# Eighty stores of an RWKV-7 layer, issued by ScalarE's queue instead of SP's

## The chip, the cores and the metric

The kernel runs on one core of one Trainium2 chip. The metric is the device time of one execution in microseconds (us); a kernel's time is the median of several executions. TensorE multiplies matrices, VectorE and ScalarE do elementwise work, GpSimd does elementwise work and some DMAs, SyncE (SP) issues most DMAs. SP and ScalarE each have a DMA queue of their own.

## What is computed

A trunk of two layers for 512 positions with a width of 2048, in float32. Layer 0 is a hybrid attention; the change lies in layer 1, an RWKV-7 time mixing. Cut to what matters:

```python
def rwkv7_mixer(h, mu, w_r, w_k, w_v, w_z, w_o, w0, w1, w2, a0, a1, a2, k_k, k_a, ...):
    xx = shifted(h) - h
    xr, xw, xk, xv, xa, xz = [h + xx * mu[i] for i in range(6)]
    r, k, v, z = xr @ w_r, xk @ w_k, xv @ w_v, xz @ w_z
    w = -softplus(-(w0 + tanh(xw @ w1) @ w2)) - 0.5
    decay = exp(-exp(w))
    a = sigmoid(a0 + (xa @ a1) @ a2)
    kk = normalised per head of (k * k_k)
    k = k * (1 + (a - 1) * k_a)
    # per position: state = state * decay + (state @ -kk) (kk * a)^T + v k^T;  y = state @ r
    ...
    return (norm(y) + bonus) * silu(z) @ w_o
```

## The kernel before

Everything is kept with the 2048 features on partitions, as 16 blocks of 128 ("pairs" of two heads of 64), and the 512 positions along the free dimension. A float32 product is made of three matmuls, `mm3` (L116 to L118): each operand is split into a high and a low half. For a weight tile of 128 x 1024, `wload` (L103) issues its load on SP's queue into a `raw` buffer (two of them), ScalarE makes the high half `wh` (L85) and VectorE the low half `wl` (L86), into three buffers each. Weight tiles are numbered through the program; `wh556` is the high half of tile 556.

The stage around the change is the dense part of layer 1, in the trace from 1203 to 1640 us. The generator `dense()` runs the projections with keys (`rwk`), values (`rwv`), receptances (`rwr`) and gates (`rwz`), one block of 128 outputs after another, each of two weight tiles. After each block a function takes the result from PSUM: `stash` for a key block (L915 copies it to `vf`, L916 stores it to `kpd` in HBM), `values` for a value block (L1014 and L1015, to `vfd`). Between these matmuls run the pieces of `pair(p)`, which is the elementwise work of one block of heads. It loads the keys back (L931), squares and normalises them, and computes decays and rates in one long run of ScalarE operations, from `th` (L950) over `ep` (L957) and `em` (L959) to `km` (L967) and `sq`; a text below calls that run the burst of a pair. L960 stores the decays `ep` to `epd`. VectorE forms the products `bk` and `kk` (L977 to L982), stored by SP at L980 and L983. `values` also orders, six ticks later, a `turn()`: TensorE transposes the value block (L1020), ScalarE copies it to `vt` (L1022, a single buffer), and two DMAs store it to `vtd` (L1025). `rates` (L1032) and GpSimd's later stages read `epd`, `vfd` and `vtd` back. `ahead(k)` prepares inputs of the gates (`hin`, `mx`, `xz`, stored at L1010 to `xzd`), and a triangular inverse per four pairs copies its results `pu` to `u4` (L906).

What runs when on TensorE is written by hand: `fill` advances one tick at a time, a tick runs what is due (`at(n, f)`) and then one `mm3` of the dense stream.

```python
tc.manual_schedule(engines={mybir.EngineType.PE})
def fill(n):
    for _ in range(n):
        for f in due.pop(now[0], ()):
            f()
        next(stream, None)
        now[0] += 1
```

The order of the other engines, SP's and ScalarE's queues included, is found by the framework's scheduler. DMAs of SP and ScalarE report their landing to one of eight counters, which the two queues share.

Of the kernel before, what the change touches and what calls it, by code (L numbers as in the profile page):

```python
# [18 lines left out]
P = 128  # L19
# [29 lines left out]
def _trunk(ctx, tc, d, out):  # L49
    nc = tc.nc  # L50
# [26 lines left out]
    def v_(name, i=0, n=1):  # L77
        o = VEC[name] + i
        return vec[:, o:o + n]
# [4 lines left out]
    def split(hi, lo, src):  # L84
        nc.scalar.activation(hi, src, AF.Copy)  # L85
        nc.vector.tensor_tensor(lo, src, f32(hi), op=ALU.subtract)  # L86
# [23 lines left out]
    def bdmm(ps, mat, hi, lo):  # L110

        nc.tensor.matmul(ps, mat, hi, start=True, stop=False)
        nc.tensor.matmul(ps, mat, lo, start=False, stop=True)

    def mm3(ps, ah, al, bh, bl, start, stop_):
        nc.tensor.matmul(ps, ah, bh, start=start, stop=False)  # L116
        nc.tensor.matmul(ps, al, bh, start=False, stop=False)  # L117
        nc.tensor.matmul(ps, ah, bl, start=False, stop=stop_)  # L118
# [115 lines left out]
    with ExitStack() as st0:  # L234
# [14 lines left out]
        for k in range(KT):  # L249
            ada.scale_shift(0, k)  # L250
            t = tp.tile([P, S], F32, tag="t", name=f"t{k}")
# [10 lines left out]
        for j in range(8):  # L262
            t = tp.tile([P, S], F32, tag="t", name=f"lt{j}")
# [12 lines left out]
    with ExitStack() as L0:  # L276
# [285 lines left out]
        with ExitStack() as ml:  # L562
# [68 lines left out]
            def attend(head, vh, vl, qrh, qrl, qk, sz):  # L631
# [31 lines left out]
                nc.sync.dma_start(yd[8 + head], y)  # L663

            nxt = pair(0), [proj(0)]
            for hp in range(4):
                pv_, qk = nxt
# [9 lines left out]
    with ExitStack() as so:  # L677
# [6 lines left out]
        for k in range(KT):  # L684
            t = y2.tile([P, S], F32, tag="yl_", name=f"yld{k}")
            nc.sync.dma_start(t, yd[k])
            a = yp.tile([P, S], R32, name=f"yh{k}")
            b = yp.tile([P, S], R32, name=f"yl{k}")
# [21 lines left out]
    NP, NC_, C = KT, 8, 64  # L710
# [3 lines left out]
    epd, vfd, y2d, z2d = (scr(n, NP, P, S) for n in ("epd", "vfd", "y2d", "z2d"))  # L714
    vtd = scr("vtd", NP, C, NC_, P)
    kpd = scr("kpd", NP, P, S)
# [30 lines left out]
    def sigmoid(t):  # L747

        nc.scalar.activation(t, t, AF.Ln, bias=1.0)
        nc.scalar.activation(t, t, AF.Exp, scale=-1.0)  # L750
# [39 lines left out]
    with ExitStack() as kp:  # L790
# [14 lines left out]
        with pool(name="sp", bufs=2) as sp:  # L805
# [3 lines left out]
            for k in range(KT):  # L809
                h = sp.tile([P, S + 1], F32, tag="h", name=f"hn{k}", bufs=3)  # L810
                nc.gpsimd.memset(h[:, 0:1], 0.0)
                t = sp.tile([P, S], F32, tag="t", bufs=4, name=f"t1_{k}")
# [22 lines left out]
        for i in range(2):  # L835
            t = lp.tile([96, S], F32, tag="lt", name=f"lt{i}")
# [33 lines left out]
        def store(g, U):  # L870
            T = kw.tile([64, 32, 32], F32, tag="t11", name=f"T{g}", bufs=1)
            nc.gpsimd.tensor_copy(T, U[:64].rearrange("p s t -> p t s"))
            nc.gpsimd.dma_start(unu[g], U.rearrange("p s t -> p (s t)"))
            nc.gpsimd.dma_start(unt[g], T.rearrange("p s t -> p (s t)"))
# [38 lines left out]
        def stash(p, ps):  # L913
            t = T_("vf", p)
            nc.scalar.activation(t, ps, AF.Copy)  # L915
            nc.sync.dma_start(kpd[p], t)  # L916

        def pair(p):

            vp = lambda n: v_(n, p)  # L920
            if p % 2 == 0:
                l2[p // 2] = []
                for n_ in ("rw2", "ra2"):
                    raw = lp.tile([96, 256], F32, tag="l2raw", name=f"l2raw{n_}{p}")
                    nc.sync.dma_start(raw, d[n_][:, p * P:(p + 2) * P])
                    hi = lp.tile([96, 256], R32, tag=f"l2h{n_}", name=f"l2h{n_}{p}")
                    lo = lp.tile([96, 256], R32, tag=f"l2l{n_}", name=f"l2l{n_}{p}")
                    split(hi, lo, raw)
                    l2[p // 2].append((hi, lo))
            ps = T_("kp", p)  # L930
            nc.sync.dma_start(ps, kpd[p])  # L931
            yield

            kk = T_("kk", p, bufs=3)
            nc.scalar.activation(kk, ps, AF.Identity, scale=vp("k_k"))
            sq = T_("sq", p)
            nc.scalar.activation(sq, kk, AF.Square)
            sqh, sql = (kw.tile([P, S], R32, tag=f"sq{i}", name=f"sq{i}_{p}", bufs=1) for i in range(2))
            split(sqh, sql, sq)
            yield  # L940
            cs = slice((p % 2) * P, (p % 2 + 1) * P)
            pu_ = []
            for i in range(2):
                u = pl.tile([P, S], F32, tag="pl", name=f"pl{p}{i}")
                mm3(u, *(w[:, cs] for w in l2[p // 2][i]), *lora[i], True, True)
                pu_.append(u)
            pn = pa.tile([P, S], F32, tag="pa", name=f"pn{p}")
            bdmm(pn, bdr, sqh, sql)
            th = T_("th", p, bufs=1)
            nc.scalar.activation(th, pu_[0], AF.Exp, bias=nw0[:, p:p + 1], scale=-1.0)  # L950
            sigmoid(th)
            L = th
            nc.vector.tensor_tensor_scan(L, smask, th, 0.0, op0=ALU.mult, op1=ALU.add)
            ep = T_("ep", p, (P, NC_, C + 1))
            nc.vector.memset(ep[:, :, 0:1], 1.0)
            L3 = L.rearrange("p (c t) -> p c t", t=C)
            nc.scalar.activation(ep[:, :, 1:], L3, AF.Exp, scale=-CE)  # L957
            em = T_("em", p)
            nc.scalar.activation(em, L, AF.Exp, scale=CE)  # L959
            nc.sync.dma_start(epd[p].rearrange("p (c t) -> p c t", t=C), ep[:, :, 1:])  # L960
            nc.vector.tensor_copy(dmp(p), ep[:, :, C])
            ta = T_("ta", p)
            nc.scalar.activation(ta, pu_[1], AF.Exp, bias=nw0[:, 16 + p:17 + p], scale=-1.0)
            sigmoid(ta)

            km = T_("km", p, bufs=1)
            nc.scalar.activation(km, ta, AF.Identity, bias=oka[:, p:p + 1], scale=vp("k_a"))  # L967
            nc.vector.tensor_tensor(km, ps, km, op=ALU.mult)

            nc.vector.tensor_scalar(sq, pn, 1e-24, None, op0=ALU.max)  # L970
            nc.scalar.activation(sq, sq, AF.Ln)
            nc.scalar.activation(sq, sq, AF.Exp, scale=-0.5)
            yield
            nc.vector.tensor_tensor(kk, kk, sq, op=ALU.mult)
            bk = T_("bk", p, (P, NC_, 2, C), bufs=1)
            bh = bk[:, :, 0]
            nc.vector.tensor_tensor(bk[:, :, 1], c3(km), c3(em), op=ALU.mult)  # L977
            nc.vector.tensor_tensor(bh, c3(ta), c3(kk), op=ALU.mult)
            nc.vector.tensor_tensor(bh, bh, c3(em), op=ALU.mult)
            nc.sync.dma_start(bkd[p], bk)  # L980
            kt_ = kk
            nc.vector.tensor_tensor(c3(kt_), c3(kk), ep[:, :, :C], op=ALU.mult)  # L982
            nc.sync.dma_start(krd[p, :, :, 0], c3(kt_))  # L983
            yield

            pn = pa.tile([P, S], F32, tag="pa", name=f"pat{p}")
            for c in range(NC_):
                cc = slice(c * C, c * C + C)
                for u in range(2):
                    r_ = slice(64 * u, 64 * u + 64)  # L990
                    nc.tensor.matmul(pn[r_, cc], bh[r_, c], kt_[r_, cc], start=True, stop=True)
            at_ = T_("at", p, (P, NC_, C), bufs=1)
            nc.vector.tensor_tensor(at_, pn.rearrange("p (c t) -> p c t", t=C), am[:, None, :].to_broadcast([P, NC_, C]), op=ALU.mult)
            nc.sync.dma_start(atd[p // 4, :, p % 4], at_)

            if p % 4 == 3:
                U = inverse(p // 4)
                store(p // 4, U)
                inv = inverse2(p // 4)
                for n in (70, 104, 112):  # L1000
                    at(n, lambda: next(inv, None))
# [10 lines left out]
        def values(p, ps):  # L1012
            vf = kw.tile([P, S], F32, tag="vf", name=f"vf{p}")
            nc.scalar.activation(vf, ps, AF.Copy)  # L1014
            nc.sync.dma_start(vfd[p], vf)  # L1015

            def turn():
                pt = pl.tile([P, S], F32, tag="pl", name=f"pvt{p}")
                for b in range(4):
                    nc.tensor.transpose(pt[:, b * P:(b + 1) * P], vf[:, b * P:(b + 1) * P], ident)  # L1020
                vt = kw.tile([P, S], F32, tag="vt", name=f"vt{p}", bufs=1)
                nc.scalar.activation(vt, pt, AF.Copy)  # L1022
                vv = vtd[p].rearrange("t (b a) f -> a t b f", a=2)
                for a in range(2):
                    nc.sync.dma_start(vv[a], vt[64 * a:64 * a + 64].rearrange("p (b f) -> p b f", f=P))  # L1025

            at(6, turn)

# [50 lines left out]
        def at(n, f):  # L1079
            due.setdefault(now[0] + n, []).append(f)  # L1080
# [8 lines left out]
        for j in range(NK0):  # L1089
            stash(j, acck[j])  # L1090
# [369 lines left out]
```

## Time and profile before

| | |
|---|---|
| median of three runs | 2446.71 us (2438.78 to 2450.34) |
| the profiled execution | 2447.56 us, span 2445.8 us, mean granted TensorE clock 0.966 |
| TensorE busy in the span | 2258.9 us (92%) |
| VectorE, ScalarE, GpSimd busy | 1609.8, 1021.0, 628.4 us |
| the stage with the change, 1203 to 1640 us | 437 us |

The profile is one execution on the chip. Its page lists busy times, the costliest groups of instructions and the DMA issues; the trace behind it answers more closely: the busy time of engines in a stretch, what an engine waited for, and the instructions in order of time. In a row of the timeline, the first number is the start (us from the span's start), the second the duration, and brackets give the idle time before it and what ended that. PE is TensorE, DVE VectorE, ACT ScalarE, POOL GpSimd; SPq is SP's DMA queue.

### The profile page before, as it was taken

Reading aid. Unit: us, or ns where it says so; the run is one execution under the profiler, and the core shown is the slowest. Engines: PE = TensorE matmul, PEld = TensorE weight load, DVE = VectorE, ACT = ScalarE, POOL = GpSimd, SP = SyncE. Lnnn points to the kernel's source line nnn. Section 1 sums busy time; section 2 is a strip of 40 time slices with the busy share of each in tenths; the row PEclk is TensorE's granted clock in tenths of the full one; section 3 lists DMA queues with packets and bytes.
Section 4 is the critical chain, followed back from the end, with each engine's and each line's share of the span. In section 5 each row is a group of like instructions: output and inputs, shape, how many; then the busy total and the mean of one; then the engine's idle time right before and its main releaser. Section 6 shows DMA issues by size and latency. Waiting matters only on the chain. (4 is left out here: it accounts for less than half of the span.)

```text
span 2445.8 us, 38074 instructions
## 1 busy us (share of the span) xinstructions
PE 2258.9 (92%) x14148; PEld 1755.3 (72%) x14148; DVE 1609.8 (66%) x2983; ACT 1021.0 (42%) x1809; POOL 628.4 (26%) x855
## 2 busy tenths in 40 slices
PE   6779999999998989998999889999999999997997
PEld 3567877777776877885688667777667777775786
DVE  6974577777767546727667766853566766675755
ACT  4233344444454443223476667642233444444222
POOL 1110022222231110110005455864323333310111
PEclk9999999999988999999999999999999999998998
DMA  8973554444313238835476789877558654445864
GB/s 317 326 247 117 167 165 155 162 154 158 117 47 114 64 105 301 293 126 188 157 219 207 217 264 279 268 203 205 129 143 243 176 142 130 129 133 184 297 203 138
DMA packets 224380, 452.03 MB, mean 185 GB/s; under 512 B 71489, under 2 KB 85953, under 8 KB 222913
## 3 DMA queue, kind: packets, MB, share of 16 engines
q1 hardware_dynamic: 206146, 400.30, 51.0%
q0 software_dynamic: 15744, 47.20, 7.6%
q8 instruction: 111, 1.82, 0.3%
q10 hardware_dynamic: 2304, 2.10, 0.3%
q14 instruction: 75, 0.61, 0.1%
HBM read 365.88 MB, written 83.63 MB: 184 GB/s over the span
## 5 line engine op out<-in xcount | busy, mean ns | idle before, releaser
L85 ACT ACTIVATE wh<-raw 128x1024 fp32r<-128x1024 f32 (+3 forms) x314 | 313.4, 1000 | 460.5 <-PE ps_r L118 85.6
L86 DVE TENSOR_TENSOR wl<-raw,wh 128x1024 fp32r<-128x1024 f32 (+3 forms) x314 | 372.8, 1189 | 198.1 <-ACT wh L85 192.9
L199 DVE CUSTOM_DVE_ANT_0 adaw<-adaw,sc,mod 128x512 f32<-128x512 f32 (+1 forms) x160 | 161.0, 1009 | 51.6 <-DMA adaw<-in_ada 49.0
L199 DVE CUSTOM_DVE_ANT_0 adaw<-adaw,sc,vec 128x1024 f32<-128x1024 f32 (+1 forms) x96 | 119.3, 1242 | 54.5 <-DMA adaw<-in_ada 54.4
L470 POOL TENSOR_TENSOR pcmn<-csn,cmn 128x128 f32<-128x128 f32 x48 | 25.6, 560 | 394.6 <-ACT pn L291 207.3
L116 PE MATMUL pwo<-xho,wh 128*128 128x512 f32 (+1 forms) x288 | 111.2, 386 | 10.7 <-ACT xho L85 7.7
L116 PE MATMUL ps_v<-xh,wh 128*128 128x512 f32 x256 | 106.3, 415 | 8.7 <-ACT wh L85 6.2
L116 PE MATMUL ps_r<-xh,wh 128*128 128x512 f32 x256 | 110.9, 433 | 0.9 <-ACT vf L1014 0.9
L117 PE MATMUL pwo<-xho,wl 128*128 128x512 f32 (+1 forms) x288 | 107.9, 375 | 4.2 <-DVE wl L86 4.2
L116 PE MATMUL ps_z<-xh,wh 128*128 128x512 f32 x256 | 111.4, 435 | 0.0
L117 PE MATMUL ps_v<-xh,wl 128*128 128x512 f32 x256 | 104.0, 406 | 5.2 <-DVE wl L86 5.2
L118 PE MATMUL pwo<-xlo,wh 128*128 128x512 f32 (+1 forms) x288 | 108.4, 377 | 0.0
L118 PE MATMUL ps_v<-xl,wh 128*128 128x512 f32 x256 | 103.9, 406 | 0.3 <-DVE xl L745 0.3
L116 PE MATMUL pw<-yh,wh 128*128 128x512 f32 x256 | 102.0, 399 | 1.9 <-ACT yh L85 1.7
L118 PE MATMUL ps_r<-xl,wh 128*128 128x512 f32 x256 | 103.8, 405 | 0.0
L117 PE MATMUL ps_r<-xh,wl 128*128 128x512 f32 x256 | 103.3, 404 | 0.0
L117 PE MATMUL pw<-yh,wl 128*128 128x512 f32 x256 | 102.5, 401 | 0.3 <-DVE wl L86 0.3
L118 PE MATMUL pw<-yl,wh 128*128 128x512 f32 x256 | 100.5, 396 | 2.0 <-DVE yl L86 2.0
L118 PE MATMUL ps_z<-xl,wh 128*128 128x512 f32 x256 | 101.4, 396 | 0.0
L117 PE MATMUL ps_z<-xh,wl 128*128 128x512 f32 x256 | 101.2, 396 | 0.0
L867 POOL TENSOR_TENSOR U<-U,Ut 128x30 f32<-128x30 f32 (+14 forms) x120 | 96.1, 801 | 9.1
L865 POOL TENSOR_TENSOR Ut<-U 128x30 f32<-128x30 f32 (+14 forms) x120 | 91.2, 760 | 9.1
(466 smaller groups left out, 6217.8 us busy)
## 6 DMA issues: line engine op xcount, KB each, us to landing
adaw<-in_ada SPq DMA_DIRECT2D x128, 512.0 KB, 6.9
adaw<-in_ada SPq DMA_DIRECT2D x128, 256.0 KB, 3.1
raw<-in_win_b SPq DMA_DIRECT2D x58, 512.0 KB, 3.6
raw<-in_rwo SPq DMA_DIRECT2D x36, 512.0 KB, 4.5
raw<-in_wout SPq DMA_DIRECT2D x32, 512.0 KB, 4.8
raw<-in_rwv SPq DMA_DIRECT2D x32, 512.0 KB, 5.0
raw<-in_rwr SPq DMA_DIRECT2D x32, 512.0 KB, 5.0
raw<-in_rwz SPq DMA_DIRECT2D x32, 512.0 KB, 4.0
```

Of the source, the lines that this page charges most:

```text
L85: nc.scalar.activation(hi, src, AF.Copy)
L86: nc.vector.tensor_tensor(lo, src, f32(hi), op=ALU.subtract)
L116: nc.tensor.matmul(ps, ah, bh, start=start, stop=False)
L117: nc.tensor.matmul(ps, al, bh, start=False, stop=False)
L118: nc.tensor.matmul(ps, ah, bl, start=False, stop=stop_)
L199: nc.vector.tensor_tensor_reduce(w, w, self.sc[:, i - self.i0:i - self.i0 + self.n], 0.5, v_("ada_b", layer * 48 + j) if i == 0 else m, op ...
L470: nc.gpsimd.tensor_tensor(pcm[:, :, r], cs, cm[:, 3][:, :, None].to_broadcast([P, 4, 32]), op=ALU.mult)
L865: nc.gpsimd.tensor_tensor(tv, U[:, :s_, s_:s_ + 1].to_broadcast([P, s_, n]), U[:, s_:s_ + 1, s_ + 1:].to_broadcast([P, s_, n]), op=ALU.mult)
L867: nc.gpsimd.tensor_tensor(U[:, :s_, s_ + 1:], U[:, :s_, s_ + 1:], tv, op=ALU.add)
```

## The change

Four lines of code issue their DMAs on ScalarE's queue (`nc.scalar.dma_start`) and no longer on SP's (`nc.sync.dma_start`): the stores of keys (L916, 16 times), decays (L960, 16), values (L1015, 16) and turned values (L1025, 32), 80 DMAs in all. What they copy, and all operations, stay.

```diff
@@ stash
             nc.scalar.activation(t, ps, AF.Copy)
-            nc.sync.dma_start(kpd[p], t)
+            nc.scalar.dma_start(kpd[p], t)
@@ pair
             nc.scalar.activation(em, L, AF.Exp, scale=CE)
-            nc.sync.dma_start(epd[p].rearrange("p (c t) -> p c t", t=C), ep[:, :, 1:])
+            nc.scalar.dma_start(epd[p].rearrange("p (c t) -> p c t", t=C), ep[:, :, 1:])
@@ values
             nc.scalar.activation(vf, ps, AF.Copy)
-            nc.sync.dma_start(vfd[p], vf)
+            nc.scalar.dma_start(vfd[p], vf)
@@ turn
                 for a in range(2):
-                    nc.sync.dma_start(vv[a], vt[64 * a:64 * a + 64].rearrange("p (b f) -> p b f", f=P))
+                    nc.scalar.dma_start(vv[a], vt[64 * a:64 * a + 64].rearrange("p (b f) -> p b f", f=P))
```

The scheduler orders VectorE, ScalarE and SP anew. TensorE keeps its order row for row, GpSimd too. ScalarE has 1727 rows instead of 1660, SP 1031 instead of 1096 (equal rows that follow one another count as one). At the start of the stage `wh556`, which stood ahead of `lh1`, a table load, `vf2` and `vf3` on ScalarE, now stands behind these and behind the stores of `vf0` to `vf3`. Three more places, before and after:

ScalarE around the split of weight tile 589. `vf` is a block of values, `vt` a turned one, `th`, `ta`, `ep`, `em`, `km` and `sq` with a 10 belong to the burst of pair 10, `xz` and `mx` to `ahead`, `kk11` to pair 11. Before:

```order
L85 ACTIVATE wh588_13149<-raw588_13148 128x1024
L937 ACTIVATE sq11_13250<-kk11_13248 128x512
L744 ACTIVATE xz0_6_13177<-mx5_6_13179 128x512
L1014 ACTIVATE vf5_13060<-ps_v1_5_12895 128x512
L85 ACTIVATE wh589_13197<-raw589_13196 128x1024
L742 ACTIVATE mx5_7_13285<-hin5_7_13280,omu_9912 128x512
L744 ACTIVATE xz0_7_13283<-mx5_7_13285 128x512
L1022 ACTIVATE vt5_13105<-pvt5_13100 128x512
L950 ACTIVATE th10_13126<-pl100_13115,nw0_9914 128x512
L749 ACTIVATE th10_13126<-th10_13126 128x512
```

The split of tile 589 stood ahead of the turned block `vt5` and of the whole burst of pair 10. In the changed kernel, on ScalarE, at the end of that burst:

```order
L971 ACTIVATE sq10_13054<-sq10_13054 128x512
L957 ACTIVATE ep10_13131<-th10_13126 128x8x64
L959 ACTIVATE em10_13134<-th10_13126 128x512
L960 DMA epd_9897<-ep10_13131 1024x1x64
L967 ACTIVATE km10_13142<-ta10_13138,oka_9916,vec_60 128x512
L972 ACTIVATE sq10_13054<-sq10_13054 128x512
L1014 ACTIVATE vf6_13192<-ps_v1_6_13063 128x512
L85 ACTIVATE wh589_13197<-raw589_13196 128x1024
L1015 DMA vfd_9898<-vf6_13192 128x512
L85 ACTIVATE sq0_11_13252<-sq11_13250 128x512
L85 ACTIVATE wh590_13272<-raw590_13271 128x1024
```

It now comes after the burst, one moved store and `vf6`; `xz0_7` comes after it.

VectorE around the low half of weight tile 598, before:

```order
L993 TENSOR_TENSOR at12_13984<-pat12_13967,c1_9910 128x512
L977 TENSOR_TENSOR bk13_14080<-km13_13825,em13_13817 128x8x64
L978 TENSOR_TENSOR bk13_14080<-ta13_13821,kk13_13739 128x8x64
L86 TENSOR_TENSOR wl598_14097<-raw598_14095,wh598_14096 128x1024
L906 COPY u4_10686<-pu_10_13993 32x16x32 x2
L906 COPY u4_10686<-pu_11_14028 32x16x32 x2
L979 TENSOR_TENSOR bk13_14080<-bk13_14080,em13_13817 128x8x64
```

The low half stood ahead of the copies of the inverse (`u4`) and of the last product of `bk13`. In the changed kernel, on VectorE:

```order
L86 TENSOR_TENSOR sq1_14_14092<-sq14_14089,sq0_14_14091 128x512
L906 COPY u4_10686<-pu_10_13993 32x16x32 x2
L906 COPY u4_10686<-pu_11_14028 32x16x32 x2
L86 TENSOR_TENSOR l2lra214_13928<-l2rawra214_13925,l2hra214_13927 96x256
L979 TENSOR_TENSOR bk13_14080<-bk13_14080,em13_13817 128x8x64
L982 TENSOR_TENSOR kk13_13739<-kk13_13739,ep13_13814 128x512
L86 TENSOR_TENSOR wl598_14097<-raw598_14095,wh598_14096 128x1024
```

It now comes after all four copies and after two products of pair 13.

SP around the load of weight tile 586 (`bkd`, `krd`, `xzd` and `utd` are stores, `hin` and `kp` loads), before:

```order
L980 DMA bkd_9896<-bk8_12847 128x1024
L983 DMA krd_9895<-kk8_12511 1024x1x64
L1010 DMA xzd0_9925<-xz0_4_12985 128x512
L1015 DMA vfd_9898<-vf4_12892 128x512
L1010 DMA xzd1_9926<-xz1_4_12986 128x512
L103 DMA raw586_12994<-in_rwv 128x1024
```

The load stood behind the stores of `bk8`, `kk8`, `vf4` and of both halves of `xz` 4. In the changed kernel, on SP:

```order
L103 DMA raw585_12896<-in_rwv 128x1024
L907 DMA utd_9904<-u4_10686 128x2048
L1010 DMA xzd0_9925<-xz0_2_12707 128x512
L1010 DMA xzd1_9926<-xz1_2_12708 128x512
L1006 DMA hin5_4_12982<-hd_9894 128x512
L103 DMA raw586_12994<-in_rwv 128x1024
L1006 DMA hin5_5_13079<-hd_9894 128x512
L931 DMA kp10_12980<-kpd_9902 128x512
L994 DMA atd_9903<-at7_12745 128x512
```

It now stands ahead of the stores of pair 8 (which follow further down), and behind those of `xz` 2.

## Rows read from the trace of the kernel before

**Rows 1.** Engines by stretch: busy us (instructions), clock, DMA share, GB/s.

```profile
core 0: us, PE busy (x) PEld busy (x) DVE busy (x) ACT busy (x) POOL busy (x), PEclk, DMA share, GB/s
1203.00:1220.00 17.00, 14.98 (x61) 10.72 (x60) 4.07 (x7) 10.30 (x14) 0.00 (x0) 1.00 0.55 167
...
1420.00:1440.00 20.00, 15.12 (x63) 11.75 (x62) 11.51 (x18) 13.60 (x24) 9.97 (x17) 0.93 1.00 291
1440.00:1460.00 20.00, 18.94 (x102) 14.69 (x102) 15.34 (x20) 11.10 (x18) 18.32 (x22) 0.90 0.67 213
...
1580.00:1600.00 20.00, 17.32 (x88) 12.95 (x87) 11.69 (x19) 8.70 (x14) 7.92 (x9) 0.83 0.96 251
...
1203.00:1640.00 437.00, 410.67 (x2862) 325.27 (x2861) 301.96 (x419) 287.81 (x457) 212.19 (x266) 0.97 0.79 235
```

**Rows 2.** TensorE's waits from 1203 to 1640 us: total, times, longest.

```profile
PE ps_v L116 <- ACT wh L85: 6.2, 2, 4.1
PE ps_v L117 <- DVE wl L86: 5.2, 3, 3.9
```

**Rows 3.** Timeline of SP's queue: raw loads 586 and 606, and a store.

```profile
1427.33 0.42 SPq L103 DMA_DIRECT2D raw<-in_rwv  x1
...
1576.56 1.38 SPq L1025 DMA_DIRECT2D vtd<-vt  x2
...
1579.89 0.43 SPq L103 DMA_DIRECT2D raw<-in_rwv  x1
```

**Rows 4.** The four lines of stores: issue, ns min/median/max, first and last start.

```profile
L916 SPq DMA_DIRECT2D kpd<-vf x16: 319/320/1185, 1210.6 to 1345.5; - x16
L960 SPq DMA_DIRECT2D epd<-ep x16: 519/536/710, 1232.3 to 1565.2; - x16
L1015 SPq DMA_DIRECT2D vfd<-vf x16: 319/360/1991, 1367.9 to 1605.3; - x16
L1025 SPq DMA_DIRECT2D vtd<-vt x32: 510/602/1360, 1388.6 to 1623.6; - x32
```

**Rows 5.** Page, DMA issues: a weight load, KB each, median us to landing.

```profile
raw<-in_rwv SPq DMA_DIRECT2D x32, 512.0 KB, 5.0
```

**Rows 6.** Timeline of ScalarE: splits of tiles 556 and 557.

```profile
1214.68 1.06 ACT L85 ACTIVATE wh<-raw 128x1024 fp32r<-128x1024 f32 x1 [2.17 <-DMA raw<-in_rwk]
...
1218.62 1.05 ACT L85 ACTIVATE wh<-raw 128x1024 fp32r<-128x1024 f32 x1
```

**Rows 7.** Timeline of ScalarE: tiles 559, 560; 589; `xz`; 590.

```profile
1226.12 1.06 ACT L85 ACTIVATE wh<-raw 128x1024 fp32r<-128x1024 f32 x1 [1.32 <-DMA raw<-in_rwk]
...
1234.47 1.04 ACT L85 ACTIVATE wh<-raw 128x1024 fp32r<-128x1024 f32 x1
...
1448.34 1.05 ACT L85 ACTIVATE wh<-raw 128x1024 fp32r<-128x1024 f32 x1
...
1454.42 0.63 ACT L744 ACTIVATE xz<-mx 128x512 fp32r<-128x512 f32 x1 [4.36 <-DVE ep L955]
...
1463.39 2.07 ACT L85 ACTIVATE wh<-raw 128x1024 fp32r<-128x1024 f32 x2
```

**Rows 8.** Timeline of VectorE and TensorE: low half 559, its first use.

```profile
1227.21 1.23 DVE L86 TENSOR_TENSOR wl<-raw,wh 128x1024 fp32r<-128x1024 f32 x1 [3.40 <-ACT wh L85]
...
1235.57 0.40 PE L116 MATMUL ps_k<-xh,wh 128*128 128x512 f32 x1
```

**Rows 9.** The same: low half 589, its first use.

```profile
1451.73 1.61 DVE L86 TENSOR_TENSOR wl<-raw,wh 128x1024 fp32r<-128x1024 f32 x1
...
1462.45 0.40 PE L116 MATMUL ps_v<-xh,wh 128*128 128x512 f32 x1
```

**Rows 10.** The same: low half 598, what follows it, its first use.

```profile
1531.23 1.47 DVE L86 TENSOR_TENSOR wl<-raw,wh 128x1024 fp32r<-128x1024 f32 x1
1532.62 2.77 DVE L906 COPY u<-pu 32x512 f32<-32x512 f32 x4
1535.42 0.69 DVE L979 TENSOR_TENSOR bk<-bk,em 128x512 f32<-128x512 f32 x1
...
1534.68 0.39 PE L116 MATMUL ps_v<-xh,wh 128*128 128x512 f32 x1
```

## The prediction, before the result was known

> **What bounds the kernel now.** All 80 stores are issued in one stage, 1203 to 1640 us, in which layer 1 forms its projections; so I read that stretch first, by engine. TensorE is busy for 410.7 of its 437 us, VectorE for 302, ScalarE for 288, and the DMA engines are at a share of 0.79 [rows 1]. TensorE bounds the stage and has 26.3 us of idle time in it. ScalarE, which takes the stores, has 437 - 288 = 149 us of idle time, but not always where it is wanted. The waits of TensorE come next: 6.2 us went on two waits for the high half of a weight tile (`wh`, split by ScalarE) and 5.2 us on three for the low half (`wl`, by VectorE) [rows 2]. The reader should see that the path runs through the weight splits: raw load by SP, `wh` on ScalarE, `wl` on VectorE, then TensorE.
>
> Two of these stalls begin on SP's queue. The load of raw tile 586 was issued at 1427.33, behind stores and other DMAs of the order shown above, and TensorE stood in the window from 1420 to 1440 (15.12 of 20 us busy). The load of tile 606 was issued at 1579.89, behind a `vtd` store of 1576.56, and TensorE stood in the window from 1580 to 1600 (17.32 busy) [rows 1, 3]. The granted clock after them is below full: 0.93 and 0.90 in the two windows from 1420 on, 0.83 in the one from 1580. An idle time of 2.0 us in the first 17 us of the stage left it at 1.00 [rows 1].
>
> **The change, part by part.** *Issue.* By the medians, 16 x 0.32 + 16 x 0.54 + 16 x 0.36 + 32 x 0.60 = 39 us of issuing leave SP and come to ScalarE [rows 4]. On SP this is time in front of loads; on ScalarE it is time in front of splits. In sum ScalarE's 149 us of slack cover it. Only a store directly ahead of a late split costs TensorE anything; some of these are counted below, and for the rest I add a tenth, 3 us after rounding down.
>
> *Wait before the store.* No row shows what a ScalarE store waits after the operation that fills its tile, on ScalarE itself. Below, it is nothing, since SP waited for the same tiles. Above, a store could stand as long as one landing: each DMA reports to one of eight counters that SP and ScalarE share, in the compiled order 48 of the 80 moved stores wait on such a counter, and a weight load takes 5.0 us to land [rows 5]. I take zero, since these stores are issued one burst apart and mostly after that landing, and keep the other end for a rival.
>
> *The order of ScalarE and VectorE moves with it.* TensorE's order does not. I found the tiles whose split moves back behind something long, and set the shift against the margin that the split had in the trace.
> - Start. `wh556` began at 1214.68 after 2.17 us of waiting for its load. The next split began at 1218.62, so 1218.62 - 1214.68 - 1.06 = 2.88 us of other work (`lh1`, the table, two `vf`) lay between them [rows 6]. In the new order that work and four stores (4 x 0.32 = 1.3) stand ahead of `wh556`: 2.9 + 1.3 - 2.2 = **2.0 us** late, with no margin.
> - `wh559`. It began at 1226.12; the burst of pair 0 that now stands ahead ended at 1234.47, and one store of 0.54 comes with it: 8.9 us later [rows 4, 7]. The low half was done at 1227.21 + 1.23 = 1228.44, TensorE used the tile from 1235.57: a margin of 7.1 [rows 8]. Loss **1.8**. `wh561` stands to the burst of pair 1 in the same way: 1.8 again, as an estimate from the same rows.
> - `wh589`. It began at 1448.34 and moves behind pair 10 and `vf6`, whose end let the next split start at 1463.39; with the store this is 15.6 us. The 4.36 us for which ScalarE stood ahead of that burst, waiting for VectorE, drop out, since the waiting operation now comes after the burst: 11.2 [rows 7]. The margin was 1462.45 - (1451.73 + 1.61) = 9.1 [rows 9]. Loss **2.1**; `wh600`, moved behind pair 14 in the same way, 2.1 again.
> - `wl598`, on VectorE. It had 1534.68 - (1531.23 + 1.47) = 2.0 us of margin. Ahead of it stand now four copies of 2.77, `bk` of 0.69 and one product more, taken at 0.69: 4.2 us [rows 10]. Loss **2.2**; `wl587`, moved back by 7 places behind another pair's products, taken as 2.2.
>
> Sum of losses: 2.0 + 3.6 + 4.2 + 4.4 = 14.2 us.
>
> *What is gained.* The loads of tiles 586 and 606 stand 8 and 4 places further forward on SP. I give the change both stalls: 6.2 us of `wh`, and 5.2 less the longest single wait of 3.9, which is another tile's, so 6.2 + 1.3 = **7.5 us** [rows 2, 3].
>
> *The clock.* The 0.83 from 1580 to 1600 costs 20 x 0.17 = 3.4 us; 0.93 and 0.90 after 1420 cost 1.4 + 2.0 = 3.4 too [rows 1]. If both stalls go, 6.8 us come back. The seven new stalls are about 2 us each; in the rows one idle time of 2.0 us cost no clock and one of 2.7 (17.32 of 20 busy) did. I let two of seven cost it, another 6.8, so the two cancel.
>
> *Sum.* 14.2 - 7.5 + 6.8 - 6.8 + 3 = 9.7, about **+10 us**. The profiled execution took 2447.56 us (span 2445.8), 0.85 over the median of the runs shown, 2446.71. So 2446.7 + 10 = **2457 us** on the scale of the median. 0.5% of it, about what a measurement of this kernel can tell from no change, is 12.2 us: the forecast is just within, and its own range is 2447 to 2468.
>
> **The rivals.**
> *Nothing on the path moves.* The margins worked out above run from 2 to 9 us [rows 8 to 10], and a stall early on hands its length to the split that comes next, so the losses need not add up. The stalls gone and the new ones then come out even, at 2447. The Trainium skill bears on this (DMA: Bandwidth & Descriptors, section Issuing engines are not separate DMA queues): starting transfers from several engines saves only the time that a sequencer needs to start them, since all run on the same 16 DMA engines. By that the sum would be no more than SP's 39 us of issue, on an engine that is not the bound; the DMA share of 0.79 in rows 1 does not speak against it, and nothing in this stage shows SP busy with issuing alone. Against it speak the late raw loads [rows 3], which are late in the queue, not in the issuing.
>
> *Faster: the relief of SP wins.* The place is SP's queue ahead of raw loads, the price the two stalls with their clock, 7.5 + 6.8 = 14.3 us. It decides if the displaced splits keep within 2 us of their margins, as they do if ScalarE's bursts start earlier than in the old order by what it had been waiting (4.36 us before pair 10 alone [rows 7]). Then 2447.56 - 14.3 = 2433. The same page of the Trainium skill has a rule for it, in the section Queues, rings and completion order: SP and ScalarE own a row of rings each, and a DMA engine takes from the rows in turn, so a load no longer stands behind SP's stores. No row here shows two such rows at work in this stage.
>
> *Slower by more: ScalarE is held by landings.* The place is the counters that the two queues share. If 16 of the 48 stores stand 2.5 us each, half a weight load's landing [rows 5], ScalarE loses 40 us in pieces; with half of them in front of a split without margin this is 20 us on top of the 10, **2477**. It decides from the point where a hold is longer than a margin, which is 2 us at `wl598` and 9 at `wh589`. For it: `wh556` stood waiting for its landing [rows 6]. Against it: the issue is spread over 400 us.
>
> That the stores do not move is excluded: the new order has 67 rows more on ScalarE and 65 fewer on SP.
>
> **How the numbers follow.** Forecast 0.45 (of it 0.18 over the 12.2 us, 0.27 within); nothing moves 0.20; faster 0.18 (0.16 beyond, 0.02 within); held by landings 0.17. So faster 0.16, same 0.27 + 0.20 + 0.02 = 0.49, slower 0.18 + 0.17 = 0.35. The range from 2432 to 2476 leaves out about half of the faster and half of the held case, 0.18 in all.
>
> **What would show it.** In the changed profile's stage I expect TensorE's wait for `wh` to fall at 1420 to 1440 and 1580 to 1600 and new waits of about 2 us at the seven tiles named; SP's waits for ScalarE to vanish from these four lines; ScalarE's busy time unchanged near 288 us; the stage from 437 to about 447 us. Wrong would be a stage under 430 us (the losses were covered), or waits of ScalarE in front of the stores of more than 20 us in sum (the landings hold it), or a change of the time that lies outside this stage, for which I have no term.

## The result and the profile after

The changed kernel takes 2466.1 us (median of 6 runs, 2464.6 to 2469.6), against 2446.4 us of the kernel before in the same job: a ratio of 1.0074, with a 95% interval from 1.0056 to 1.0092. It is slower, by 18 us by the ratio and 19.7 by the medians. The forecast was 2457 with a range from 2432 to 2476: the range holds the result, the sign of the sum was right, and its size, 10 us, was half of what came.

The page of the changed kernel's profile, its span and first part:

```profile
span 2463.4 us, 38059 instructions
...
PE 2261.5 (92%) x14148; PEld 1753.0 (71%) x14148; DVE 1604.0 (65%) x2983; ACT 1023.9 (42%) x1809; POOL 625.5 (25%) x855
```

To set the two traces side by side I cut both at the same work, from the first matmul with weight tile 555 (with the wait ahead of it) to the first with tile 640: 4876 matmuls in each. Busy time by engine, clock, DMA share; first the kernel before:

```profile
1209.13:1893.57 684.44, 646.55 (x4876) 501.77 (x4877) 438.32 (x690) 352.50 (x571) 309.10 (x408) 0.97 0.75 216
```

and the changed kernel:

```profile
1203.32:1911.89 708.57, 653.77 (x4876) 505.57 (x4877) 433.34 (x690) 355.57 (x571) 304.30 (x408) 0.96 0.73 208
```

The same work takes 24.1 us more. TensorE is idle for 708.6 - 653.8 = 54.8 us instead of 37.9, so 16.9 us more, and its busy time is 7.2 us longer for the same matmuls, at a lower mean granted clock (0.96 against 0.97). (Ahead of this stretch the two executions differ by 5.8 us the other way, in code that the change doesn't touch; over the traces of this study the stretch begins anywhere from 1203 to 1211 us. The medians carry 19.7.)

TensorE's waits in the changed kernel, from 1203 to 1660 us, total, times, longest:

```profile
PE ps_v L117 <- DVE wl L86: 12.3, 6, 3.1
PE ps_r L117 <- DVE wl L86: 5.8, 1, 5.8
PE ps_v L116 <- ACT wh L85: 5.0, 3, 2.0
PE ps_k L116 <- ACT wh L85: 3.9, 1, 3.9
...
PE ps_k L117 <- DVE wl L86: 1.8, 3, 0.8
```

Where before 6.2 us were lost on `wh` and 5.2 on `wl` [rows 2], and 0.3 more on a `wl` of the keys, it is now 8.9 on `wh` and 19.9 on `wl`, of which 3.1 at tile 579 is the 3.9 of before. The waits for weight halves have grown by 28.8 - 11.7 = 17.1 us, which is all of the 16.9. In order of time, TensorE's rows that begin with such a wait (the idle time before it stands in brackets) are these. They belong to tiles 556, 559, 561, 587, 589 (two rows), 595, 598, 600 (two) and 610:

```profile
1214.54 0.50 PE L116 MATMUL ps_k<-xh,wh 128*128 128x512 f32 x1 [3.86 <-ACT wh L85]
...
1236.84 0.50 PE L117 MATMUL ps_k<-xh,wl 128*128 128x512 f32 x1 [0.70 <-DVE wl L86]
1250.49 0.50 PE L117 MATMUL ps_k<-xh,wl 128*128 128x512 f32 x1 [0.34 <-DVE wl L86]
...
1449.65 0.50 PE L117 MATMUL ps_v<-xh,wl 128*128 128x512 f32 x1 [3.07 <-DVE wl L86]
1466.75 0.50 PE L116 MATMUL ps_v<-xh,wh 128*128 128x512 f32 x1 [2.05 <-ACT wh L85]
1468.49 0.80 PE L117 MATMUL ps_v<-xh,wl 128*128 128x512 f32 x1 [1.24 <-DVE wl L86]
1515.27 0.50 PE L116 MATMUL ps_v<-xh,wh 128*128 128x512 f32 x1 [1.60 <-ACT wh L85]
...
1547.88 0.50 PE L117 MATMUL ps_v<-xh,wl 128*128 128x512 f32 x1 [2.84 <-DVE wl L86]
1562.75 0.49 PE L116 MATMUL ps_v<-xh,wh 128*128 128x512 f32 x1 [1.34 <-ACT wh L85]
1564.49 0.80 PE L117 MATMUL ps_v<-xh,wl 128*128 128x512 f32 x1 [1.25 <-DVE wl L86]
1646.48 0.80 PE L117 MATMUL ps_r<-xh,wl 128*128 128x512 f32 x1 [5.83 <-DVE wl L86]
```

All seven tiles that the prediction named are there, and two that it didn't, 595 and 610. At 586 and 606 no wait is left. How the wait at 589 comes about shows on ScalarE, first and last rows of the burst of pair 10:

```profile
1457.97 0.69 ACT L950 ACTIVATE th<-pl,nw 128x512 f32<-128x512 f32 x1 [1.48 <-PE pl L118]
...
1465.17 0.58 ACT L1014 ACTIVATE vf<-ps_v 128x512 f32<-128x512 f32 x1
1465.65 1.04 ACT L85 ACTIVATE wh<-raw 128x1024 fp32r<-128x1024 f32 x1
```

The load of 589 had landed at 1455; its split stood in the queue for 10 us, and TensorE waited 2.05 us for it. In [rows 7] it ran at 1448. On VectorE the low half of 598 waits in the same way behind the copies of the inverse:

```profile
1541.87 2.77 DVE L906 COPY u<-pu 32x512 f32<-32x512 f32 x4
...
1545.41 0.68 DVE L979 TENSOR_TENSOR bk<-bk,em 128x512 f32<-128x512 f32 x1
1546.01 0.68 DVE L982 TENSOR_TENSOR kk<-kk,ep 128x512 f32<-128x512 f32 x1
1546.61 1.21 DVE L86 TENSOR_TENSOR wl<-raw,wh 128x1024 fp32r<-128x1024 f32 x1
```

These are the 4.2 us of work that the prediction had put there from [rows 10].

The stores now stand on ScalarE's queue, and take there what they took on SP's [rows 4] (issue, ns min/median/max, first and last start):

```profile
L916 ACTq DMA_DIRECT2D kpd<-vf x16: 325/327/355, 1204.8 to 1346.8; - x16
L960 ACTq DMA_DIRECT2D epd<-ep x16: 526/534/597, 1229.4 to 1583.6; - x16
L1015 ACTq DMA_DIRECT2D vfd<-vf x16: 325/326/1692, 1370.6 to 1621.8; - x16
L1025 ACTq DMA_DIRECT2D vtd<-vt x32: 515/542/2118, 1395.7 to 1642.5; - x32
```

### The profile page after: what moved, and what is told of

The parts are those of the page before. It is cut to its first block, busy times and chain, and to the rows that moved or that the text cites. A ratio compares the mean times of both kernels' runs of the same rounds, so it can differ in the third digit from the quotient of the medians.

```text
span 2463.4 us, 38059 instructions
## 1 busy us (share of the span) xinstructions
PE 2261.5 (92%) x14148; PEld 1753.0 (71%) x14148; DVE 1604.0 (65%) x2983; ACT 1023.9 (42%) x1809; POOL 625.5 (25%) x855
```

## Experiments

Two theories were on record. **A**: the scheduler, given other stores on ScalarE, found another order for ScalarE, VectorE and SP, in which weight splits come later; that order is the loss. **B**: a store on ScalarE costs by itself, by its issue or by a landing that it waits for. To part them, some kernels pin an order. A table `ORDER` lists, by engine, the instructions of the stage, and each is tied behind the one ahead of it on its engine by an edge that fixes the order of issue and adds no wait. The 80 stores are left out of the table, so they find their own places between:

```diff
-        assert not due
+        assert not due; pin(tc, nc)
...
+def pin(tc, nc):
+    seen = {i.name: i for i in nc.cur_bb.bb.instructions}
+    info = mybir.DependencyInfo(mybir.DependencyClass.NoSync, mybir.DependencyReason.DATA)
+    for o in ORDER.values():
+        for a, b in zip(o, o[1:]):
+            tc.add_manual_dep(seen[f"I-{b + 10668}"], f"I-{a + 10668}", info, reason="order")
```

Each ratio below is to the kernel before on the same chip in the same job, with its 95% interval.

**Stores moved, order kept.** The changed kernel with the order of the kernel before in `ORDER`.

> The four lines of stores go to ScalarE as in the change, but every other instruction of ScalarE, VectorE and SP in the stage keeps the place that it had before the change (edges of order pin them); only the stores are placed anew. Theory A (the loss comes from the weight splits that the scheduler moved back): TensorE's waits of about 2 us at tiles 556, 559, 561, 589, 595, 598 and 600 are gone, and the time is that of before or a little less, 2438 to 2450 us. Theory B (a store on ScalarE costs by itself, by its issue, or by the landing for which it stands): the loss stays, 2460 to 2470 us.

Measured: 2448.3 us, ratio 1.0014 [1.0000, 1.0029]. The waits at 559, 561, 587, 589, 595, 600 and 610 are gone, that at 556 is as small as before; one of 1.5 us is left at 598, and the stalls of 586 and 606 are back. A's number. All 80 stores on ScalarE cost at most 7 us here, 3.4 by the ratio and 1.3 by the medians of this job.

**Stores kept, order changed.** The kernel before with the order of the changed kernel.

> The reverse: all stores stay on SP's queue, and ScalarE, VectorE and SP are pinned to the order of the changed kernel. Theory A: the waits at tiles 559, 561, 589, 598 and 600 are there without any store on ScalarE, 2456 to 2470 us. Theory B: no loss, 2440 to 2450 us.

Measured: 2467.8 us, ratio 1.0095 [1.0076, 1.0114], the whole loss without one store on ScalarE. TensorE's waits from 1203 to 1660 us in this kernel:

```profile
PE ps_v L117 <- DVE wl L86: 11.2, 6, 3.5
PE ps_v L116 <- ACT wh L85: 5.9, 3, 3.3
PE ps_r L117 <- DVE wl L86: 5.8, 1, 5.8
...
PE ps_k L116 <- ACT wh L85: 3.3, 1, 3.3
```

They are those of the changed kernel, within 1.1 us a group. With the run above this is a square of two by two, and the order explains all of the loss that the intervals can tell from nothing.

**Single lines.** In each of the next five runs some of the four lines are changed as in the full diff and the others stay on SP; the scheduler is free. Values:

```diff
-            nc.sync.dma_start(vfd[p], vf)
+            nc.scalar.dma_start(vfd[p], vf)
```

> Only the 16 stores of values (L1015) move to ScalarE. In the order that results, the splits of tiles 586 and 598 come 16 and 19 places earlier on ScalarE, the load of 606 5 places earlier on SP, and no split comes 4 or more places later there. Theory A: the two stalls of 4.9 and 2.7 us of the kernel before go, nothing takes their place, with the clock 2430 to 2442 us, faster than before. Theory B: 16 of 80 stores, a fifth of the loss, 2448 to 2452 us.

Measured: 2444.8 us, ratio 0.9997 [0.9983, 1.0010]. Theory A's number was missed: the stalls of 586 and 606 did go, and yet nothing was gained. In their place TensorE waited for copies of value blocks (5.6 us on `ps_r` for `vf`, 0.9 before). This opened the question of the two runs with splits moved by hand, below.

Decays:

```diff
-            nc.sync.dma_start(epd[p].rearrange("p (c t) -> p c t", t=C), ep[:, :, 1:])
+            nc.scalar.dma_start(epd[p].rearrange("p (c t) -> p c t", t=C), ep[:, :, 1:])
```

> Only the 16 stores of decays (L960) move to ScalarE. In the order that results the splits of tiles 589 and 600 come 14 and 16 places later on ScalarE and those of 587, 589, 598 and 600 5 to 11 places later on VectorE; those of 556, 559 and 561 keep their places, and 586 comes 14 places earlier. Theory A: waits of 2 to 4 us at 587, 589, 598 and 600, none at 556, 559 and 561; less the stall at 586, 2450 to 2462 us. Theory B: a fifth of the loss, 2448 to 2452 us, with no new wait of TensorE over 1 us.

Measured: 2445.7 us, ratio 1.0003 [0.9989, 1.0017]: a miss for the number of A, too. The waits stand where A put them, at 587, 589, 598 and 600, but the stalls of 586 and 606 went: on the halves of the value tiles TensorE waited 3.3 + 8.7 = 12.0 us in its trace, against 6.2 + 5.2 = 11.4 before [rows 2], and the two come out even.

Keys:

```diff
-            nc.sync.dma_start(kpd[p], t)
+            nc.scalar.dma_start(kpd[p], t)
```

> Only the 16 stores of keys (L916) move to ScalarE. In the order that results the splits of tiles 556, 559 and 561 come 4, 13 and 14 places later on ScalarE, and nothing changes after 565. Theory A: waits at these three tiles of 1 to 4 us and no others new; by the prediction's terms 2.0 + 1.8 + 1.8 = 5.6 us, 2449 to 2456 us with or without the clock. Theory B: a fifth of the loss, 2448 to 2452 us, and no new wait at 559 and 561.

Measured: 2454.2 us, ratio 1.0032 [1.0016, 1.0048], 7.8 us slower, where the prediction's terms for these tiles give 5.6. Of the three waits only that of 556 is large:

```profile
PE ps_k L116 <- ACT wh L85: 3.8, 1, 3.8
```

With the low halves of 556 and 559, 0.9 us, this is 4.7 of the 7.8. In the cut of the result section TensorE's idle time is 6.1 us longer than before in this trace, and its busy time 2.8. No split behind tile 565 moves by more than three places, so this is the cleanest of the single lines.

Turned values:

```diff
-                    nc.sync.dma_start(vv[a], vt[64 * a:64 * a + 64].rearrange("p (b f) -> p b f", f=P))
+                    nc.scalar.dma_start(vv[a], vt[64 * a:64 * a + 64].rearrange("p (b f) -> p b f", f=P))
```

> Only the 32 stores of turned values (L1025), the longest to issue, move to ScalarE. In the order that results 586, 587 and 598 come 13 to 18 places earlier on ScalarE, 606 5 places earlier, and none over 6 places later there; on VectorE 601 and 610 come 8 places later. Theory A: 2440 to 2450 us, with what is gained at 586 handed on as in the kernel with two splits earlier. Theory B: 32 of 80 stores, 2452 to 2456 us.

Measured: 2453.1 us, ratio 1.0027 [1.0011, 1.0043]. By its number this is B's, but not by its trace: TensorE's largest single wait in it is at tile 610, one of the two tiles that I had not named.

```profile
PE pvt L1020 <- ACT vf L1014: 7.3, 3, 3.9
PE ps_r L117 <- DVE wl L86: 6.8, 1, 6.8
```

Tile 610's low half came 8 places later on VectorE; the two rows together are 14.1 us against 3.2 us for the first group before. But the stalls of 586 and 606 are gone here, and in the same cut as above TensorE is idle for only 1.6 us and busy for 0.9 us more than before. So this trace does not show where the 6.6 us of the runs come from.

Decays, values and turned values together, by the same three diffs:

> The decays, values and turned values (64 stores) move to ScalarE, the keys stay on SP. In the order that results 556, 559 and 561 keep their places; 587, 589, 595, 598, 600 and 610 come as late as in the full change, 586 and 606 as early. Theory A: the loss of the full change (18 us by its ratio) less that of the keys alone (8 us), so about 10 us, 2452 to 2460 us. If only combinations with the keys cost: 2445 to 2449 us.

Measured: 2458.4 us, ratio 1.0056 [1.0035, 1.0077], 13.7 us. With the 7.8 of the keys this makes 21.5, a little over the 18 of the full change; the sum of the four single lines, 7.8 + 0.7 - 0.7 + 6.6 = 14.4, is a little under it. Each of these numbers is uncertain by 3 to 5 us, so the losses add up as far as the runs can tell. They do not go by the number of stores: 16 stores of keys cost 7.8 us, 16 of values nothing.

**The gain by itself.** The prediction credited the change with two stalls and their clock, 14.3 us. The kernel before with its own order pinned, but for tiles 586 and 606; of the edit, ScalarE's places:

```diff
 ORDER (places in the table)
-  ... vf4 th9 ... em9 ... vt4 wh586
+  ... vf4 wh586 th9 ... em9 ... vt4
-  xh0_2 ... mx0_4 xh0_4 wh606
+  wh606 xh0_2 ... mx0_4 xh0_4
```

> The kernel before, all stores on SP, its order pinned, with two weight tiles moved forward: the loads of 586 and 606 by 7 and 4 places on SP, their high halves by 14 and 5 on ScalarE, their low halves by 7 and 4 on VectorE. The term of the prediction for what the change gains (two stalls of 7.5 us and the clock after them, 6.8 us): 2430 to 2438 us. Rival (the next late split or operand stops TensorE instead, so the gain is handed on): 2443 to 2448 us.

Measured: 2445.6 us, ratio 0.9999 [0.9985, 1.0013]. The rival has it: both stalls are gone (0.73 us came at 587), and nothing is gained. The same cut as in the result section, from tile 555 to 640:

```profile
1204.84:1892.61 687.77, 641.24 (x4875) 497.58 (x4876) 437.85 (x690) 353.01 (x571) 305.51 (x408) 0.98 0.75 215
```

TensorE is busy for 5.3 us less than before, so of the 6.8 us of clock most came back in this trace (two traces of one order, before and with its stores moved, differ by 2.5 us in this). But it is idle for 46.5 us instead of 37.9, though 7.5 us of stalls went. Its waits over the stage:

```profile
PE pvt L1020 <- ACT vf L1014: 9.2, 3, 4.8
PE ps_r L116 <- ACT vf L1014: 7.5, 1, 7.5
```

and ScalarE and TensorE at the second of them:

```profile
1599.29 0.72 ACT L742 ACTIVATE mx<-hin,omu 128x512 f32<-128x512 f32 x1 [5.65 <-DMA hin<-hd]
1599.92 0.58 ACT L1014 ACTIVATE vf<-ps_v 128x512 f32<-128x512 f32 x1
...
1600.55 0.80 PE L116 MATMUL ps_r<-xh,wh 128*128 128x512 f32 x1 [7.46 <-ACT vf L1014]
```

The copy `vf` that TensorE needs stands behind `mx`, which waits 5.65 us for its input. In the kernel before, ScalarE stood at the same `mx` for nearly as long, but TensorE, later itself, did not wait for this copy:

```profile
1598.68 0.72 ACT L742 ACTIVATE mx<-hin,omu 128x512 f32<-128x512 f32 x1 [5.18 <-DMA hin<-hd]
```

With its stalls gone TensorE met the next operation in ScalarE's queue that was behind a load. Counted from the start of the cut, this `mx` also runs 4.9 us later than before. So the edit, which puts the load of 606 ahead of others on SP, may have delayed that load as well; the runs do not separate the two.

The third tile, 579, by the same edit (`wh579` ahead of `th6`, `wl579` ahead of the VectorE work of pair 6):

> The same with a third tile, 579, whose two halves move ahead of the burst of pair 6 (17 places on ScalarE, 16 on VectorE), where TensorE waited 3.9 us and the clock fell to 0.83. If stalls and their clock add up: 7 us under the kernel with two tiles, about 2425 us. Rival: the inputs of the values come as late as before and the wait is handed to them, no more than 3 us under it.

Measured: 2450.3 us, ratio 1.0018 [1.0004, 1.0032]. Again the rival, and if anything a loss; the wait for `wl579` is gone from its trace, and TensorE waits 10.5 us for `vf` at its transposes, 3.2 before. And with the stores on ScalarE:

> The changed kernel, all 80 stores on ScalarE, with the same pinned order and the same three tiles forward. Theory A: within 5 us of the same order with the stores on SP. Theory B: 15 to 20 us above it.

Measured: 2449.5 us, ratio 1.0017 [1.0004, 1.0031], 0.8 us from the same order with the stores on SP.

**A version that could beat both.** From the trace of the kernel with two splits earlier I took the time at which each weight load, each half of a split and each copy of a value block had its operands from tile 581 on, and pinned each there. 

> All stores on SP; from tile 581 on the order of ScalarE, VectorE and SP is pinned so that each weight load, both halves of each split and each copy of a value block stand where their operands were ready in the trace of the kernel with two splits earlier, ahead of bursts and of inputs that wait for loads. If TensorE was held only by the places of these operations: its waits for splits and value copies from 581 to 610 (13 to 20 us in the kernels so far) fall under 5 us, 2428 to 2438 us. Rival: the bursts and inputs that now come later hold TensorE instead, 2442 to 2450 us.

Measured: 2461.2 us, ratio 1.0060 [1.0039, 1.0080], outside the rival's range too, on the slow side. The low halves are ready 8 to 20 us before TensorE needs them at most tiles, and what the splits were moved past holds TensorE, the copies of turned values and of the inverse:

```profile
PE pl L116 <- ACT vt L1022: 12.0, 2, 9.8
PE pu L904 <- ACT inv2v L897: 6.8, 1, 6.8
```

> The same pinned order with all 80 stores on ScalarE. Theory A: within 5 us of the same order with the stores on SP. Theory B: 15 to 20 us above it.

Measured: 2462.6 us, ratio 1.0062 [1.0044, 1.0080]. No kernel of this study is measurably faster than the one before.

Four orders have now been run with the stores on either queue:

| order of ScalarE, VectorE and SP | stores on SP | stores on ScalarE |
|---|---|---|
| of the kernel before | 2446.4 us (1) | 2448.3 us (1.0014) |
| of the changed kernel | 2467.8 us (1.0095) | 2466.1 us (1.0074) |
| of before, three tiles earlier | 2450.3 us (1.0018) | 2449.5 us (1.0017) |
| splits as early as their operands | 2461.2 us (1.0060) | 2462.6 us (1.0062) |

In brackets is the ratio to the kernel before in the same job; the first two rows set runs of two jobs side by side. In a row the two medians differ by 0.8 to 1.9 us, with either sign, and the ratios by about 5 us at most, where each is uncertain by 3 to 5 us. Down a column it is up to 21 us. The queue that issues the stores costs or gains nothing that these runs can see. The order is the change.

## Why the prediction was right, and where it was not

*What bounds the stage* held: the path runs through the weight splits, and the loss stands mostly in TensorE's waits for them, 17.1 of the 24.1 us.

*Order as the mechanism* held. It was the forecast's own, and the two-by-two runs show it. Tile by tile, the sum of the rows above against the terms (both halves taken together): 556: 3.86 and 0.76 more for the low half, 4.6 against 2.0; 559 and 561: 0.7 and 0.3 against 1.8 each; 587: 3.1 against 2.2; 589: 3.3 against 2.1; 598: 2.8 against 2.2; 600: 2.6 against 2.1. That is 17.4 us against 14.2; 0.3 of it, at 556, was there before.

*The term of the start* was too small because of a wait that I had not put there. In the new order `vf2` stands ahead of `wh556`, and it waited for the landing of the first store of keys, which had gone out at 1204.8. This is not the queue's doing: with the stores on SP, in the same order, it waited as long. The changed kernel first, then the run with the stores kept:

```profile
1211.82 1.21 ACT L915 ACTIVATE vf<-ps_k_pi 128x512 f32<-128x512 f32 x2 [3.16 <-DMA kpd<-vf]
```

```profile
1214.20 1.21 ACT L915 ACTIVATE vf<-ps_k_pi 128x512 f32<-128x512 f32 x2 [3.08 <-DMA kpd<-vf]
```

In the kernel before, `vf2` came after `wh556`, at 1217.57, and did not wait.

*Two tiles were missing*, 595 (1.60 and 0.76) and 610 (5.83), 8.2 us together. I had looked for splits moved behind bursts of pairs, and tile 610 is moved behind the copies of the last inverse, as 598 is. This is the largest miss of the sum among the waits.

*The clock* was let to cancel; by TensorE's busy time it cost 7.2 us (4.6 between the two pinned runs of the square, 653.6 against 649.0). Windows of 20 us with a wait in them, in the changed kernel:

```profile
1200.00:1220.00 20.00, 13.77 (x48) 9.48 (x47) 4.55 (x7) 12.89 (x18) 0.00 (x0) 0.91 0.58 185
...
1440.00:1460.00 20.00, 16.93 (x95) 13.22 (x94) 13.82 (x19) 10.99 (x19) 17.90 (x27) 0.91 0.98 303
1460.00:1480.00 20.00, 16.71 (x94) 12.69 (x93) 17.15 (x16) 13.46 (x21) 18.43 (x21) 0.91 0.63 188
...
1500.00:1520.00 20.00, 17.64 (x97) 13.64 (x96) 11.67 (x20) 13.24 (x22) 2.15 (x4) 0.90 1.00 299
...
1540.00:1560.00 20.00, 17.16 (x196) 13.78 (x196) 13.56 (x21) 10.92 (x20) 18.51 (x20) 1.00 0.78 258
1560.00:1580.00 20.00, 17.41 (x90) 13.26 (x89) 16.58 (x17) 9.74 (x14) 18.51 (x20) 0.83 0.68 211
...
1640.00:1660.00 20.00, 14.17 (x49) 10.96 (x48) 13.60 (x16) 7.30 (x10) 18.35 (x22) 0.83 0.58 181
```

I had let two of the seven waits named lower it. It is lower in the windows of four of them (556, 587, 589, 600) and of both tiles that I had not named (595, 610). It is 1.00 in that of 598, whose wait was 2.84 us, and in those of 559 and 561, with waits under 1 us.

*The gain of 7.5 us* is there in the waits that went, at 586 and 606, and in the changed kernel the waits add up: 25.3 us are new, 8.3 are gone (0.8 of it at 579), and TensorE's idle time grew by 16.9. But that the relief would be a gain of time by itself, and with the clock 14.3, failed: two splits earlier give 0. The rival on the faster side fell with it, and so did the number expected of the values alone. There the waits had been taken as if each were paid once, while one taken away brought another, of copies that stood behind a load. That the range holds the result owes something to its width: the clock, let to cancel, and the two missing tiles are 15.4 us that the sum did not have.

*The rest of 3 us for a longer queue on ScalarE* is not seen. In four rows of the table the medians put it between -1.7 and +1.9.

*The other rivals.* "Nothing moves" fell by the interval, 1.0056 at its low end. "Held by landings" stayed far from its 40 us. The waits of ScalarE that a landing of these stores ended, in the changed kernel over the stage, are 6.9 us:

```profile
ACT vf L915 <- DMA kpd<-vf: 5.0, 2, 3.2
...
ACT vt L1022 <- DMA vtd<-vt: 1.9, 2, 1.4
```

They are waits of copies and not of stores, and with the stores on SP in the same order they are 4.9. A hold in front of a store, as the rival has it, is there in the run with the stores moved and the order kept: one store of `ep` left 1.8 us after `em`, at 1524.66, and ScalarE stood idle for 2.3 us until the landing of a store of `vt`. (Ahead of 37 of the 80 stores the trace of the changed kernel has a wait of their own; the prediction had 48 from the compiled order.)

The Trainium skill's rule (DMA: Bandwidth & Descriptors, section Issuing engines are not separate DMA queues), that starting transfers from several engines saves only the time to start them, agrees with the table: 80 stores on another queue changed the medians by less than 2 us either way in the same order. What it cannot say is what a scheduler makes of the same edit.

Open: why an order that is earlier for every split is 15 us slower is told by two rows of waits, and was not tried further; nor was an order sought for all engines at once.

## What to carry to other kernels

Where a scheduler orders the queues, an edit to a DMA's engine is an edit to the order: compare the orders first, and read, for each operation on the critical path, what it now stands behind and what margin it had. Then hold the order fixed on either side of the edit; a pair of such runs tells what the edit itself is worth, here less than they can tell from nothing. And a wait that a trace shows is not a gain to be had: try it by itself before it enters a sum, since the operation behind it in the queue may be waiting for a load of its own.

## What the runs showed that was not expected

Issue on ScalarE's queue takes 0.33 to 0.54 us a store by the medians, 0.32 to 0.60 on SP's. 80 of them between the operations of an engine that is busy for two thirds of the stage leave no clear trace in the time: 1.0014 with an interval that begins at 1.0000, in the same order. Nor did relief of SP help. With 39 us of issuing taken off it, SP stood longer ahead of weight loads, waiting for VectorE to free a buffer. From 1197 to 1664 us, in the changed kernel:

```profile
SPq L103 <- DVE wl L86: 89.8, 41, 9.2
```

With the stores kept on SP in the same order it is 58.8 us, and the other rows of the table go the same way: 59.0 us became 69.0 in the order of before, 48.9 became 66.8 with three tiles earlier, 61.5 became 105.9 with the splits early. A queue with less to issue waited longer here for the splits that free its buffers.
